# Strassen's scheme for the second token half of an encoder layer's input projection

## The chip, the cores and the metric

One core of one Trainium2 chip. The time is the device time of one execution in microseconds (us). The kernel is float32 throughout. Engines are named as the profile names them: PE is the tensor engine (PEld its weight loads), DVE the vector engine, ACT the scalar engine, POOL the GpSimd engine, SP the engine that issues most of the DMAs.

## The reference

One layer of a transformer-like encoder on 2048 tokens of width 1024 (`BATCH` 1, `DEPTH` 1), cut to what matters:

```python
h = rms_norm(x, norm_mix[l])
z = h @ w_in[l]                       # 1024 -> 4352
q_a, k_a, v_a, q_b, k_b, v_b, g_a, g_b = jnp.split(z, offsets, axis=-1)
                                      # 512, 128, 128, 512, 512, 512, 1024, 1024
y_a = windowed_gqa(q_a, k_a, v_a, sink[l])      # 8 heads on 2 kv heads, |t-s| <= 128, ALiBi
y_b = neighborhood_attn(q_b, k_b, v_b, rpb[l])  # 8 heads, 32 x 64 token grid, 8 x 16 window
gates = jax.nn.sigmoid(jnp.concatenate([g_a, g_b], axis=-1) + b_gate[l])
merged = gates[..., :D_MODEL] * (y_a @ w_proj_a[l]) + gates[..., D_MODEL:] * (y_b @ w_proj_b[l])
x = x + merged @ w_out[l]
x = x + jnp.square(jax.nn.relu(rms_norm(x, norm_mlp[l]) @ w_up[l])) @ w_down[l]
return rms_norm(x, norm_final)
```

## The kernel before

**Products in three parts.** Each float32 operand is split into a high and a low half (`split`, L234 to L236: ACT casts the high half, DVE or POOL subtracts it). Each 128 x 128 x 512 product is three matmuls, high-high, high-low and low-high (`mm3` at L193 to L195, `mm3s` at L239 to L241).

**Blocks and pages.** Tokens come in four blocks of 512 (0 to 3). The normalised input of a block is kept with features on partitions; a page is one half of the 1024 features for one block, 512 x 512, as a high and a low tile. A feature tile is 128 of the 4352 output columns.

**First token half: Strassen quads.** Blocks 0 and 1 are projected by a Winograd form of Strassen's scheme. `in_quad` (L407) takes two neighbouring groups of columns, `w` wide each (128 or 256), and both blocks; it makes seven products in the order `ORDER = (1, 2, 5, 6, 7, 4, 3)`, each of 12 matmuls for each of `w / 128` tiles. The left operands are sums of weight blocks (`in_left`, tiles `zS`, `zwhl`), the right ones seven pages `in_page[n]` (tiles `zh1` to `zh7`), made once from x. DVE adds the products up in `zc` tiles. The list of quads is

```python
QUADS = [(O_KA, P), (O_QA, 256), (O_QB, 256), (O_KB, 256), (O_VB, 256)]
QUADS += [(O_GA + n * BT, 256) for n in range(4)]
```

The first is a key and a value tile of attention A, the last four are the gates. `in_result` (L388) takes a finished tile: queries and keys are split once more (`qk_parts`, into an `in_e()` buffer, tile `ze`), values are transposed by PE and split (`v_parts`, L350 and L351, into `in_v2()`, tile `zv`, one buffer), and all are stored to DRAM by SP (`qs_a`, `ks_a`, `vs_a`, `qs_b`, `ks_b`, `vs_b`, `zg` for gates). Beside quads 4 and 5 (O_VB and the first gates) blocks 2 and 3 of x are normalised, transposed and stored to `h1d` (L448, L566).

**Attention A and B, with the second half as filler.** Then `h1d` is loaded again as four pages (`hT`), and the same 34 feature tiles of blocks 2 and 3 are made without Strassen, 24 matmuls a piece (`feature_tile`): `qk_tile`, `v_tile` and `gate_tile` are generators that yield after each block. Their 68 pieces are the filler of both attentions. `paced` ties each piece to the end of an attention unit:

```python
def paced(filler, pieces, total, lag):
    for n in pieces:
        at = n * 32 // total - lag
        with tc.issue_after(done[at]) if at >= 0 else nullcontext():
            next(filler, None)
```

Attention A has 32 units: kv group `g`, query block `i` (`attn_a`). A unit makes scores (L657, L658), adds a bias and takes the maximum (DVE L659), exponentials (ACT L666), scales by the reciprocal (POOL L670), transposes (PE L676), splits the transposed weights (ACT L679, DVE L680) and multiplies by the values (L681, L682). The filler for keys and queries is needed by later units, so A runs blocks 0 to 6 of both groups first (with 12 pieces), then 7 to 15 (with 12 more). Attention B has 32 units of head and column band (`attn_b`): scores L810, bias and maximum L815, exponentials L821, scale L825, transposes of four pairs of rows L837, split L842 and L843, products L848, output L855 and L856. 20 pieces are paced over B and 24 more issued behind the first loads of the merge.

**Merge and the rest.** For each block, `load_y` (L903, L904) loads and splits both attention outputs, the projections are gated and added, `w_out` is applied and the residual added. The result is normalised, transposed (L1182), scaled by ACT into an `h2s` tile (L1184, two buffers) and stored to `h2d`. The up and down projections follow, both by Strassen's scheme over all tokens.

**Order.** The program is written in one order; a scheduler in the framework then fixes each engine's own order at build time, within the data dependences and `issue_after`. Pools of on-chip memory are opened and closed as stacks on a left and a right side, so a tile may have to wait for the last user of the place that it takes.

Of the kernel before, what the change touches and what calls it, by code (L numbers as in the profile page):

```python
# [15 lines left out]
D = 1024  # L16
# [76 lines left out]
def encoder_layer(ctx, tc, x, norm_mix, w_in, b_gate, sink, rpb, w_pa, w_pb, w_out,  # L93
# [62 lines left out]
    h1d = [dp.tile([D, BT], F32, name=f"h1d{b}") for b in range(2)]  # L156
    zg = [[dp.tile([2, D, BT], F32, name=f"zg{b}")] for b in range(NB)]
# [114 lines left out]
    in_page = {n: ring(s_z, f"zh{n}", PAGE, F32R, 2, "left") for n in (1, 2, 6)}  # L272
# [4 lines left out]
    in_v2 = ring(s_z, "zv2", [P, 1024], F32, 1)  # L277
# [4 lines left out]
    in_page[3] = ring(s_z, "zh3", PAGE, F32R, 2)  # L282
    s_kv = ExitStack()
    kvw = ring(s_kv, "kvw", [P, 4, 256], F32, 2)
# [105 lines left out]
    def in_result(col, b, src, in_psum):  # L390

        if col < O_VB and col != O_VA:
            for dst, t in qk_parts(col, b, src, in_e()):
                SY.dma_start(dst, t)
            return
        if in_psum:
            t = in_e()[:, 0]
            A.copy(t, src)
            src = t
        if is_v(col):  # L400
            for dst, t in v_parts(col, b, src, zbank(tpool, 2), in_v2()):
                SY.dma_start(dst, t)
        else:
            f = (col - O_GA) // P
            SY.dma_start(zg[b][0][f // 8, (f % 8) * P : (f % 8 + 1) * P, :], src)

    def in_quad(c, w, lf, right, ybanks=ypool, zbanks=zpool):  # L407

        na = w // P
        x, y, z = [None] * 2, [None] * 2, [None] * 2  # L410
        c1, u2, c22 = [None] * 2, [None] * 2, [None] * 2
        for n in ORDER:
            hl, (rh, rl) = next(lf), right[n]
            for a in range(na):
                if n == 1:
                    x[a] = zbank(xpool[a])
                elif n == 5:
                    z[a] = zbank(zbanks[a])
                elif n == 6:
                    y[a] = zbank(ybanks[a])  # L420
                ps = {1: x, 2: x, 5: z, 3: z, 6: y, 7: y, 4: y}[n][a]
                at = slice(a * P, (a + 1) * P)
                for k in range(4):
                    mm3s(ps, hl[:, 0, k, at], hl[:, 1, k, at], rh[:, k], rl[:, k], k == 0 and n in (1, 5, 6), k == 3)
                first, second = c + a * P, c + w + a * P
                if n == 1:
                    c1[a] = in_c()
                    A.copy(c1[a], ps)
                elif n == 2:
                    in_result(first, 0, ps, True)  # L430
                elif n == 6:
                    u2[a] = in_c()
                    add(V, u2[a], ps, c1[a])
                elif n == 7:
                    c22[a] = in_c()
                    add(V, c22[a], ps, c1[a])
                    add(V, c22[a], z[a], c22[a])
                    in_result(second, 1, c22[a], False)
                elif n == 4:
                    add(V, c1[a], ps, c1[a])  # L440
                    in_result(second, 0, c1[a], False)
                elif n == 3:
                    add(V, u2[a], ps, u2[a])
                    in_result(first, 1, u2[a], False)
            yield
# [10 lines left out]
    def row_half(c, w, p):  # L456
        t = kvw() if w == P else in_raw()
        SY.dma_start(t, w_in[0][p * BT : (p + 1) * BT, c : c + 2 * w].rearrange("(k p) f -> p k f", p=P))
        return t
# [74 lines left out]
    xp = pools(s_z, "right", ("xin", "st"), "x2")  # L534
# [15 lines left out]
    for q in range(2, len(QUADS)):  # L550
        if q == 7:
            bias_tables()
        lf = list(in_left(ws, 256))
        if q + 1 < len(QUADS):
            ws = in_weights(*QUADS[q + 1])
        if q in (4, 5):

            b = q - 2
# [18 lines left out]
    s_h = ExitStack()  # L577
    hpl = [pool(f"hT{n}", side="left", stack=s_h) for n in range(4)]
# [3 lines left out]
    hp = {}  # L582
    for b in (2, 3):
        hi, lo = [], []
        for p in range(2):
            h, l = (T(hpl[2 * (b - 2) + p], PAGE, F32R, "hT", 2) for _ in range(2))
            for n, (hh, ll) in enumerate(zip(halves(h), halves(l))):
                raw = T(wp, [P, KC, P], F32, "raw", 3).rearrange("p (k a) c -> p k (a c)", k=2)
                r = p * BT + n * 256
                SY.dma_start(raw, h1d[b - 2][r : r + 256, :].rearrange("(k p) t -> p k t", p=P))  # L590
                split(raw, hh, ll, V)
            hi.append(h)
            lo.append(l)
        hp[b] = hi, lo


    def qk_tile(col, scale, tiled=False):
        hl = slice_of([(cols(w_in[0], col), KC)])
        yield
        for b in (2, 3):  # L600
            ps = psum("mm", 2)
            feature_tile(ps, hl, hp[b])
            out = qk_parts(col, b, ps, T(wp, [P, 2, BT], F32, "z", 2))
            for dst, t in out:
                SY.dma_start(dst, t)
            yield

    def v_tile(col):
        hl = slice_of([(cols(w_in[0], col), KC)])
        yield  # L610
        for b in (2, 3):
            ps = psum("mm", 2)
            feature_tile(ps, hl, hp[b])
            vt = T(wp, [P, 2, BT], F32, "z", 2)[:, 0]
# [7 lines left out]
    dist = T(ap_, [P, 384], F32, "dist", 1)  # L622
    SY.dma_start(dist, dist_a)
    bias_a = [None] * 2

    def make_bias_a(g):
        t = T(ap_, [P, 4, 384], F32, f"biasa{g}", 1)
        for h in range(4):
            G.tensor_scalar(t[:, h], dist, 2.0 ** -(4 * g + h + 1), 1.0, ALU.mult, ALU.mult)
        bias_a[g] = t  # L630
# [80 lines left out]
    def paced(filler, pieces, total, lag):  # L711

        for n in pieces:
            at = n * 32 // total - lag
            with tc.issue_after(done[at]) if at >= 0 else nullcontext():
                next(filler, None)

    def gate_tile(f, blocks):
        hl = slice_of([(cols(w_in[0], O_GA + f * P), KC)])
        yield  # L720
        for b in blocks:
            ps = psum("mm", 2)
            feature_tile(ps, hl, hp[b])
            z = T(wp, [P, 2, BT], F32, "z", 2)[:, 0]
# [12 lines left out]
    for g in (1, 0):  # L737
        make_bias_a(g)

    live = []  # L740
    for g in (1, 0):
        load_kv(g, 0)
# [13 lines left out]
    bp = pools(s_b, "right", ("masks", "braw", "biass", "biasl", "kb0", "qb", "kb1"), "b")  # L756
    bp.update(pools(s_b, "left", ("vb", "sb", "phb", "plb", "yb", "stb"), "b"))
    boff, bstart, btotal = bias_layout()
    masks = T(bp, [P, btotal], F32, "masks", 1)
# [125 lines left out]
    s_b.close()  # L885
    s_pg = ExitStack()
    p4 = pools(s_pg, "right", ("page", "yraw", "z"), "m")

    def load_y(b):
        yh, yl = [], []  # L890
        for n in range(2):
            h = T(p4, [P, 4, BT], F32R, "page", 4)
            l = T(p4, [P, 4, BT], F32R, "page", 4)
            for c in range(4):
                raw = T(p4, [P, BT], F32, "yraw", 6)
                src = (y_a[c // 2][(c % 2) * P : (c % 2 + 1) * P] if n == 0 else y_b[c])[:, b * BT : (b + 1) * BT]
                SY.dma_start(raw, src)
# [12 lines left out]
    paced(fill, range(20, 44), 40, 4)  # L910
# [227 lines left out]
    for b in range(NB):  # L1138
# [3 lines left out]
        for f in range(8):  # L1142
            hl = slice_of([(cols(w_pa[0], f * P), 4), (cols(w_pb[0], f * P), 4)])
            parts = []
            for n in range(2):
# [3 lines left out]
                g = T(wp, [P, 2, BT], F32, "z", 2)[:, 0] if n else T(p4, [P, BT], F32, "z", 4)  # L1149
# [7 lines left out]
            if b == 0:  # L1157
                load_wo(f)
# [20 lines left out]
        for k in range(KC):  # L1179
# [3 lines left out]
            ht = T(ph2, [P, BT], F32, "h2s", 2)  # L1183
# [214 lines left out]
```

## Time and profile before

| | |
|---|---|
| median of 3 runs | 2751.87 us (2751.0 to 2756.17) |
| the profiled execution | 2750.41 us, its span 2748.6 us |
| busy share of PE, DVE, ACT, POOL | 97%, 56%, 45%, 31% |
| dense projection matmuls (L193 to L195, `mm<-hT,whl`) | 3 x 544 |
| Strassen input matmuls (L239 to L241, `zb<-zh,zwhl`) | 3 x 476 |
| granted PE clock, mean | 0.986 |
| DMA | 480.86 MB, mean 175 GB/s |

Stages by the windows of the trace: the quads run to 387 us, attention A to 710, attention B to 1112, the merge to about 1500, up to 2131, down to the end. In a window's line the first figure is its length, then each engine's busy time with its number of instructions, then the granted clock (1.00 is full), the share of DMA time and GB/s. Matmuls are pipelined: one of 512 columns is shown as 0.39 us long, but the next starts 0.23 us after it, so the distance between starts is what a matmul costs.

### The profile page before, as it was taken

What the parts mean: (1) busy time and instruction counts of PE and PEld (TensorE: products, weight loads), DVE (VectorE), ACT (ScalarE), POOL (GpSimd) and SP (SyncE); (2) the same over time, 40 slices, a digit from 0 to 9 for tenths busy, and PEclk for the clock granted to TensorE, in tenths of its full rate; (3) what the DMA queues carried; (4) which work ended last, traced back from release to release, by engine and by line L of the source; (5) the groups of instructions that cost most, each with busy time, mean ns of one, the idle gap of its engine ahead of it and who ended that gap; (6) DMA issues with size and microseconds to landing.
All of it is one profiled execution on the core that took longest, in us unless ns stands there. A gap on an engine that the chain in (4) does not pass through costs nothing.

```text
span 2748.6 us, 35115 instructions
## 1 busy us (share of the span) xinstructions
PE 2658.3 (97%) x12332; PEld 2190.2 (80%) x12332; DVE 1551.9 (56%) x2352; ACT 1250.2 (45%) x2225; POOL 839.6 (31%) x671
## 2 busy tenths in 40 slices
PE   7998998999999999899999899989999999999998
PEld 6886877777788888787887788878888888888887
DVE  8754447676454444543435567586654644546667
ACT  6343236665455555534533444554444332322444
POOL 1111223334455552433420365555544000000000
PEclk9999999999999999999999999999999999999999
DMA  4855274446677665746534656574444954445555
GB/s 148 229 152 176 98 228 141 114 115 175 179 208 199 179 172 148 234 145 197 187 107 181 224 175 201 185 228 146 143 141 161 338 179 154 145 156 173 179 183 175
DMA packets 329664, 480.86 MB, mean 175 GB/s; under 512 B 28024, under 2 KB 162296, under 8 KB 327312
## 3 DMA queue, kind: packets, MB, share of 16 engines
q1 hardware_dynamic: 300560, 445.06, 51.5%
q10 hardware_dynamic: 28928, 33.56, 3.8%
q8 instruction: 97, 1.59, 0.2%
q14 instruction: 79, 0.65, 0.1%
HBM read 323.28 MB, written 155.26 MB: 174 GB/s over the span
## 4 chain that ended last, share of the span: by engine, by line
PE 85%; DMA 6%; DVE 5%; ACT 2%; issue 1%; POOL 0%; SPq 0%; ACTq 0%; POOLq 0%; DVEq 0%
PE b L239 14%; PE b L241 14%; PE b L240 14%; PE mm L193 5%; PE mm L195 5%; PE mm L194 5%; PE zb L241 3%; PE zb L240 3%; PE zb L239 3%; PE pt L193 2%; PE pt L195 2%; PE pt L194 2%; PE av L848 2%; PE pt L837 2%; PE s L810 2%
## 5 line engine op out<-in xcount | busy, mean ns | idle before, releaser
L240 PE MATMUL b<-dwh,dah 128*128 128x512 f32 x896 | 348.5, 389 | 0.0
L241 PE MATMUL b<-dwh,dah 128*128 128x512 f32 x896 | 347.7, 389 | 0.0
L239 PE MATMUL b<-dwh,dah 128*128 128x512 f32 x896 | 338.1, 389 | 1.5 <-ACT dwh L235 1.5
L232 POOL TENSOR_TENSOR uc<-uc,uc 128x512 f32<-128x512 f32 x120 | 233.3, 1958 | 206.8 <-issue 150.1
L235 ACT CAST dah<-da 128x1024 fp32r<-128x1024 f32 (+1 forms) x128 | 121.0, 945 | 366.4 <-PE b L241 243.1
L236 DVE TENSOR_TENSOR dah<-da,dah 128x1024 fp32r<-128x1024 f32 (+1 forms) x128 | 139.3, 1089 | 221.4 <-ACT dah L235 218.3
L239 PE MATMUL b<-ubh,uwhlb 128*128 128x512 f32 x592 | 232.2, 392 | 6.2 <-ACT h2s L1184 5.4
L241 PE MATMUL b<-ubh,uwhlb 128*128 128x512 f32 x592 | 231.3, 392 | 2.6 <-DVE uwhlb L236 2.6
L240 PE MATMUL b<-ubh,uwhlb 128*128 128x512 f32 x592 | 232.0, 392 | 0.0
L193 PE MATMUL mm<-hT,whl 128*128 128x512 f32 x544 | 220.7, 406 | 4.7 <-ACT whl L175 2.4
L232 DVE TENSOR_TENSOR uc<-b,uc 128x512 f32<-128x512 f32 x160 | 109.1, 688 | 203.1 <-PE b L241 162.6
L195 PE MATMUL mm<-hT,whl 128*128 128x512 f32 x544 | 217.0, 399 | 1.2 <-POOL whl L176 1.2
L194 PE MATMUL mm<-hT,whl 128*128 128x512 f32 x544 | 216.1, 397 | 0.0
L176 POOL TENSOR_TENSOR whl<-raw,whl 128x1024 fp32r<-128x1024 f32 x66 | 159.4, 2416 | 159.2 <-ACT whl L175 138.1
L1288 POOL TENSOR_TENSOR st<-st,power 128x1 f32<-128x1 f32 x16 | 13.6, 857 | 613.6 <-DVE st L1287 613.5
L239 PEld LDWEIGHTS b<-dwh,dah 128*128 128x128 f32 x896 | 168.1, 188 | 36.7 <-ACT dwh L235 1.9
L240 PEld LDWEIGHTS b<-dwh,dah 128*128 128x128 f32 x896 | 168.2, 188 | 34.9
L241 PEld LDWEIGHTS b<-dwh,dah 128*128 128x128 f32 x896 | 168.2, 188 | 34.8
L239 PE MATMUL zb<-zh,zwhl 128*128 128x512 f32 x476 | 190.4, 402 | 3.8 <-DVE zh L451 2.6
L240 PE MATMUL zb<-zh,zwhl 128*128 128x512 f32 x476 | 189.9, 400 | 1.8 <-DVE zh L236 1.8
L241 PE MATMUL zb<-zh,zwhl 128*128 128x512 f32 x476 | 187.5, 399 | 0.6 <-DVE zwhl L236 0.5
L239 PEld LDWEIGHTS b<-ubh,uwhlb 128*128 128x128 f32 x592 | 112.1, 189 | 30.2 <-ACT h2s L1184 5.7
(241 smaller groups left out, 6235.4 us busy)
## 6 DMA issues: line engine op xcount, KB each, us to landing
at<-uc SPq DMA_DIRECT2D x224, 256.0 KB
da<-at SPq DMA_DIRECT2D x96, 512.0 KB
dw<-in_w_down_dram SPq DMA_DIRECT2D x160, 256.0 KB
uraw<-in_w_up_dram SPq DMA_DIRECT2D x32, 1024.0 KB
raw<-in_w_in_dram SPq DMA_DIRECT2D x34, 512.0 KB
zraw<-in_w_in_dram SPq DMA_DIRECT2D x16, 1024.0 KB
z<-zg SPq DMA_DIRECT2D x64, 256.0 KB
xin<-in_x_dram SPq DMA_DIRECT2D x16, 512.0 KB
```

The costliest lines, as they stand in the source:

```text
L176: G.tensor_tensor(out=hl[:, 1], in0=raw, in1=hl[:, 0].bitcast(F32), op=ALU.subtract)
L193: PE.matmul(ps, lh, rh, start=first, stop=False)
L194: PE.matmul(ps, lh, rl, start=False, stop=False)
L195: PE.matmul(ps, ll, rh, start=False, stop=last)
L232: return eng.tensor_tensor(out=out, in0=a, in1=b, op=op).ins
L235: A.copy(hi, src)
L236: eng.tensor_tensor(out=lo, in0=src, in1=hi.bitcast(F32), op=ALU.subtract)
L239: PE.matmul(ps, lh, rh, start=first, stop=False, skip_group_check=True)
L240: PE.matmul(ps, lh, rl, start=False, stop=False, skip_group_check=True)
L241: PE.matmul(ps, ll, rh, start=False, stop=last, skip_group_check=True)
L810: PE.matmul(ps[:, :n], q[:, i, :], kv[:, z, B_R0[i] // 4 : (B_R0[i] + B_NR[i]) // 4, 4 * B_C0[j] : 4 * (B_C0[j] + w)], start=z == 0, stop= ...
L837: PE.transpose(pt[:kp, at + (i - i0) * P : at + (i - i0 + 1) * P], s[i][:, rr : rr + kp], ident)
```

## The change

The second half of the tokens goes through `in_quad` too, for the first four quads (keys, values and queries of A, queries and keys of B: 14 of the 34 feature tiles). Only `v_b` (4 tiles) and the gates (16) of blocks 2 and 3 stay dense filler: 40 pieces, 22 paced over A and 18 over B. The nine quads of the first half come first, then the four of the second; between them the seven pages are replaced, in the same memory, from `h1d` and from four sums of its blocks that are made in chunks beside quads 7 and 8 and kept in DRAM. Pages 1, 2 and 3 stay for the dense filler, which needs one more page (`b12`). Attention A runs group 0 whole, then group 1; its bias, K and V tiles are placed anew. The bias distances are loaded into the bias tile itself. O_VB's quad gets two value buffers of its own, x of blocks 2 and 3 is turned beside quads 5 and 6, two feature chunks to a store. Attention B is no longer cut in two; its mask has a pool of its own. In the merge the first load of `w_out` is issued after the first load of attention output, the `z` buffers become three single ones, and the last block's h2 goes into the merge's `mh` tile, eight chunks wide, instead of `h2s`.

```diff
-    in_page = {n: ring(s_z, f"zh{n}", PAGE, F32R, 2, "left") for n in (1, 2, 6)}
+    s_h = ExitStack()
+    in_page = {n: ring(s_h, f"zh{n}", PAGE, F32R, 2, "left") for n in (1, 2, 3)}
+    in_page[6] = ring(s_z, "zh6", PAGE, F32R, 2, "left")
...
-    in_v2 = ring(s_z, "zv2", [P, 1024], F32, 1)
+    in_v2 = [ring(s_z, "zv2", [P, 1024], F32, 1)]
...
-    def in_quad(c, w, lf, right, ybanks=ypool, zbanks=zpool):
+    def in_quad(c, w, lf, right, ybanks=ypool, zbanks=zpool, b0=0):
...
-                    in_result(first, 0, ps, True)
+                    in_result(first, b0, ps, True)
...
+    in_v2.append(ring(s_v, "zv3", [P, 1024], F32, 2))
...
+    steps = [(*c, 0) for c in QUADS] + [(*c, 2) for c in QUADS[:4]]
+    n_first = len(QUADS)
+    def chunk_sums(kk):
+        b = {}
+        for j, p in ((0, 0), (1, 0), (1, 1), (0, 1)):
+            b[p, j] = chunk()
+            SY.dma_start(b[p, j], h1d[j][p * BT + kk * P : p * BT + (kk + 1) * P, :])
+        t1, t3, t2, t4 = b[0, 0], b[0, 1], b[1, 1], b[1, 0]
+        for n, o, x, y in ((5, t1, t3, t1), (7, t3, t2, t3), (6, t2, t2, t1), (4, t4, t4, t2)):
+            add(V, o, x, y, ALU.subtract)
+            SY.dma_start(h1s_d[n][kk * P : (kk + 1) * P, :], o)
+    def next_page(n):
+        src = {1: h1d[0][0:BT], 2: h1d[0][BT:D], 3: h1d[1][BT:D]}.get(n)
+        src = h1s_d[n] if src is None else src
+        hi, lo = in_page[n](), in_page[n]()
+        for m, (h, l) in enumerate(zip(halves(hi), halves(lo))):
+            t = page_raw()
+            SY.dma_start(t, src[m * 256 : (m + 1) * 256, :].rearrange("(k p) t -> p k t", p=P))
+            split(t, h, l, G if n in (4, 3) else V)
+        right[n] = (hi, lo)
-    for q in range(2, len(QUADS)):
+    for q in range(2, len(steps)):
+        c, w, b0 = steps[q]
...
-        if q in (4, 5):
+        if q in (5, 6):
...
-            for k in range(KC):
-                ps = zbank(tpool, 2)
-                turned(ps, xt, k)
-                ht = in_e()[:, 0]
-                scaled(ht, ps, k)
-                SY.dma_start(h1d[b - 2][k * P : (k + 1) * P, :], ht)
-        for _ in in_quad(*QUADS[q], iter(lf), right):
+            for k in range(0, KC, 2):
+                ht = in_e()
+                for i in range(2):
+                    ps = zbank(tpool, 2)
+                    turned(ps, xt, k + i)
+                    scaled(ht[:, i], ps, k + i)
+                SY.dma_start(h1d[b - 2][k * P : (k + 2) * P, :].rearrange("(k p) t -> p k t", p=P), ht)
+        if q in (7, 8):
+            for kk in range(2):
+                chunk_sums(2 * (q - 7) + kk)
+        for _ in in_quad(c, w, iter(lf), right, b0=b0):
             pass
+        if q == n_first - 1:
+            s_ck.close()
+            page_raw = ring(s_z, "zpr", [P, 2, BT], F32, 4)
+            for n in ORDER:
+                next_page(n)
...
-    ap_ = pools(s_a, "left", ("ka1", "va1", "qa", "sa", "ph", "pl", "ya", "sta"), "a")
-    ap_.update(pools(s_a, "right", ("dist", "biasa0", "va0", "ka0", "biasa1"), "a"))
+    ap_ = pools(s_a, "left", ("ka1", "va1", "qa", "sa", "ph", "pl", "ya", "sta", "biasa1"), "a")
+    ap_.update(pools(s_a, "right", ("va0", "ka0", "biasa0"), "a"))
...
+    hp = {2: ([right[1][0], right[2][0]], [right[1][1], right[2][1]]),
+          3: ([b12[0], right[3][0]], [b12[1], right[3][1]])}
...
-        for n in pieces:
-            at = n * 32 // total - lag
+        for n in range(pieces):
+            at = min(n * 32 // total - lag, 31)
...
-    dense = [qk_tile(O_KA, 1.0), v_tile(O_VA)]
-    dense += [qk_tile(O_QA + t * P, 0.125) for t in range(4)]
-    for t in range(4):
-        dense.append(qk_tile(O_KB + t * P, 0.125))
-        dense.append(qk_tile(O_QB + t * P, 1.0, tiled=True))
-        dense.append(v_tile(O_VB + t * P))
-    fill = chain(dense + [gate_tile(f, (2, 3)) for f in range(16)])
+    fill = chain([v_tile(O_VB + t * P) for t in range(4)] + [gate_tile(f, (2, 3)) for f in range(16)])
...
-    drive((attn_a(g, i) for g in (1, 0) for i in range(7)), live, False)
-    paced(fill, range(12), 24, 3)
-    flush()
-    for g in range(2):
-        load_kv(g, 1)
-    drive((attn_a(g, i) for g in range(2) for i in range(7, 16)), live, True)
-    paced(fill, range(12, 24), 24, 3)
+    drive((attn_a(g, i) for g in range(2) for i in range(16)), live, True)
+    paced(fill, 22, 22, 3)
...
-    units = ahead_of(all_b(), 1)
-    drive((next(units) for _ in range(15)), live, False)
-    paced(fill, range(20), 40, 4)
-    flush()
-    drive(units, live, True)
+    drive(ahead_of(all_b(), 1), live, True)
...
     first_y = load_y(0)
-    paced(fill, range(20, 44), 40, 4)
+    first_load = last_dma[0]
+    paced(fill, 18, 14, 4)
...
-                load_wo(f)
+                with tc.issue_after(first_load):
+                    load_wo(f)
...
-            ht = T(ph2, [P, BT], F32, "h2s", 2)
+            if b == NB - 1:
+                h2 = T(p4x, [P, KC, BT], F32R, "mh", 1).bitcast(F32) if k == 0 else h2
+                ht = h2[:, k]
+            else:
+                ht = T(ph2, [P, BT], F32, "h2s", 2)
```

More of the change, by code (lines that the diff above doesn't have):

```diff
@@ L156, in encoder_layer @@
     h1d = [dp.tile([D, BT], F32, name=f"h1d{b}") for b in range(2)]
+    h1s_d = {n: dp.tile([BT, BT], F32, name=f"h1sum{n}") for n in (4, 5, 6, 7)}
     zg = [[dp.tile([2, D, BT], F32, name=f"zg{b}")] for b in range(NB)]
@@ L576, in encoder_layer @@
     wp = pools(s_w, "right", ("raw", "whl", "z", "v2"), "w")
-    s_h = ExitStack()
-    hpl = [pool(f"hT{n}", side="left", stack=s_h) for n in range(4)]
+    s_m = ExitStack()
+    masks = pool("masks", side="right", stack=s_m)
+    hpl = pool("hT", side="left", stack=s_h)
     s_a = ExitStack()
-    ap_ = pools(s_a, "left", ("ka1", "va1", "qa", "sa", "ph", "pl", "ya", "sta"), "a")
-    ap_.update(pools(s_a, "right", ("dist", "biasa0", "va0", "ka0", "biasa1"), "a"))
[L582 to L606, printed above, removed]
+    ap_ = pools(s_a, "left", ("ka1", "va1", "qa", "sa", "ph", "pl", "ya", "sta", "biasa1"), "a")
+    ap_.update(pools(s_a, "right", ("va0", "ka0", "biasa0"), "a"))
+    b12 = tuple(T(hpl, PAGE, F32R, "hT", 2) for _ in range(2))
+    for n, (h, l) in enumerate(zip(*map(halves, b12))):
+        raw = T(wp, [P, KC, P], F32, "raw", 3).rearrange("p (k a) c -> p k (a c)", k=2)
+        SY.dma_start(raw, h1d[1][n * 256 : (n + 1) * 256, :].rearrange("(k p) t -> p k t", p=P))
+        split(raw, h, l, V)
+    hp = {2: ([right[1][0], right[2][0]], [right[1][1], right[2][1]]),
+          3: ([b12[0], right[3][0]], [b12[1], right[3][1]])}
     def v_tile(col):
```

56 lines of the change are left out of this document (33 added, 23 removed).

## The prediction

> **What bounds the kernel now.** First the page: how full is each engine, and who is on the chain that ended last.
>
> ```profile
> PE 2658.3 (97%) x12332; PEld 2190.2 (80%) x12332; DVE 1551.9 (56%) x2352; ACT 1250.2 (45%) x2225; POOL 839.6 (31%) x671
> ```
>
> The tensor engine (PE) is busy for 97% of the span, and the page puts 85% of the last chain on it. So time changes in two ways only: matmuls that go away, and stretches in which PE stands still. Second, the windows by stage (us, then busy us and instruction counts of PE, PEld, DVE, ACT, POOL, then the granted clock):
>
> ```profile
> 0.00:387.00 387.00, 363.65 (x1599) 292.33 (x1600) 229.12 (x278) 157.90 (x240) 65.45 (x50) 0.99 0.55 164
> 387.00:710.00 323.00, 305.08 (x1517) 248.22 (x1516) 197.79 (x537) 186.50 (x462) 122.51 (x161) 0.98 0.55 148
> 710.00:1112.00 402.00, 393.24 (x2209) 338.26 (x2208) 192.51 (x496) 214.58 (x493) 192.21 (x212) 0.99 0.66 179
> ```
>
> These are the Strassen quads of the first half, attention A, attention B. In B the vector engine (DVE) and ACT have half of the time to spare, because 936 projection matmuls lie between the attention's own. Third, the waits of PE, longest first, from 230 to 1600 us (total, times, longest):
>
> ```profile
> PE s L193 <- ACT page L903: 8.3, 1, 8.3
> PE b L239 <- ACT h2s L1184: 5.4, 1, 5.4
> ...
> PE s L810 <- DMA qb<-qs_b: 4.6, 2, 3.1
> ...
> PE zb L229 <- ACT ze L448: 3.6, 1, 3.6
> ...
> PE zb L337 <- DVE zv L351: 2.4, 1, 2.4
> ...
> PE zb L229 <- DVE zv L351: 1.9, 1, 1.9
> ```
>
> These are joints between stages. A joint costs more than its wait, since a half-speed clock follows it. I call "lost" whatever a stretch takes beyond its matmuls at their usual distance from start to start (in the timeline 0.23 us for 512 columns, 0.177 for 384, 0.118 for 256, 0.109 for a transpose). By that count the span loses 137 us: 12 from 200 to 300 (v stores), 14 where A starts (387 to 430), 12 where B starts (700 to 740), 12 where the merge starts (1112 to 1130), 11 where the up projection starts (1500 to 1535).
>
> Fourth, single units of attention (windows from one unit's last product to the next one's):
>
> ```profile
> 459.20:467.10 7.90, 5.76 (x33) 4.83 (x32) 5.92 (x11) 4.37 (x8) 2.66 (x2) 1.00 0.52 135
> 467.10:470.50 3.40, 3.40 (x13) 2.99 (x11) 3.13 (x12) 1.99 (x8) 0.00 (x0) 0.50 0.35 90
> 533.70:540.00 6.30, 5.71 (x28) 3.79 (x28) 5.56 (x18) 4.74 (x13) 0.70 (x1) 1.00 0.70 187
> 540.00:548.30 8.30, 8.30 (x43) 6.87 (x43) 3.48 (x11) 5.06 (x13) 4.54 (x8) 1.00 0.13 38
> 641.50:648.10 6.60, 5.60 (x31) 3.93 (x29) 6.57 (x19) 4.72 (x13) 5.18 (x8) 1.00 0.64 169
> ```
>
> The third and fifth have no projection matmul in them, the first has 6, the fourth 24. Their own matmuls come to 4.4 to 5.3 us at the usual distances, so these thin units lose 1.9, 2.1 and 2.6; the filled one loses nothing. In a thin unit DVE is busy nearly throughout (6.57 of 6.60): PE waits for its own softmax. Of A's 29 units after the first, 5 are thin (at most 6 projection matmuls) and lose 1.97 each on average; the others lose 0.46. In B no unit has less than 24 (mean loss 0.3). This is the view that the change must be read by.
>
> **The parts.**
>
> *Matmuls gone.* 14 feature tiles x 2 token blocks x 24 matmuls = 672 dense ones become 7 products x 12 matmuls x 7 tile pairs = 588. 84 fewer x 0.231 us = -19.4. The Strassen quads run at the same distance as dense tiles (0.231 in both), so this is nearly certain. Their splits, sums and stores lie beside PE: the quads of the first half lose 0.1 to 0.2 us in 50 where no joint is near.
>
> *Filler gone from B.* What moves out of the attentions is their cover: 28 of 68 projection pieces. The order of the changed kernel's PE shows where the 40 pieces left stand: in A 8 thin units of 29, in B 17 of 31 with no filler at all and 14 with 24. No thin unit of B is in the trace, so I work one out. From the end of the transposes of its first pair, ACT makes one copy (0.48), then the four exponentials of a later unit, which stand next in its order:
>
> ```profile
> 735.88 0.54 ACT L821 ACTIVATE sb<-sb,stb 128x288 f32<-128x288 f32 x1 [1.75 <-DVE stb L818]
> ...
> 738.13 0.46 ACT L842 CAST phb<-pt 128x384 fp32r<-128x384 f32 x1
> ```
>
> 2.25 us for the narrow columns; 2 x (0.709 - 0.606) + 2 x (0.606 - 0.530) = 0.36 more for the wide ones, so 2.4. Then the copy of the previous output (0.5), DVE's sum of it (0.6, ACT's next copy beside it), DVE's low half (0.69): 4.8 with semaphores. PE meanwhile has four score matmuls and four products of the unit before (1.2), eight transposes (0.87), four scores (0.6) and four products (0.47): 3.1. It waits 1.7, with two smaller steps 2.0, as in A's rows. DVE needs 172 us for 30 units from 740 to 1090, at most 5.7 each, against 4.86 of PE: at least about 1 is lost per thin unit. Upper bound 3.5 (A's worst, 2.6, times four pairs over three chunks). I take 2.0, the hand sum and A's mean row together. So B loses 17 x 2.0 + 14 x 0.46 = 40 against 10 now: +31 (between +14 and +56). A: 8 x 1.97 + 21 x 0.46 = 25 against 21: +4 (0 to +10).
>
> *v stores.* O_VB's quad had one v buffer: ACT waited 29 us in it for stores. Now it has two, and the transposed x moves into the gate quads, in half as many stores. Of 12 lost, 9 go (4 to 12).
>
> *Start of A.* K and V of group 0 now lie where the last quad's weight halves lay, so their loads wait for that quad's last matmul. On SP four stores stand between them (0.57 us from issue to issue in the timeline of the v stores), so the last key half is issued near 4 us and, with 3 to 4.8 us to land (4.8 in the chain at 375), is there at 7 to 9; 24 projection matmuls (5.5) cover that but for some 2. The four page loads and splits ahead of the first dense tile become one. Two almost bare units follow as before. 14 lost become 8: -6 (-12 to +6).
>
> *Start of B.* Keys of B's first head come where A's group 0 was, long free; but its score tiles overlie A's last values, so PE still waits for one softmax: -3 (-8 to +5).
>
> *Start of the merge.* Two filler pieces (48 x 0.231 = 11.1 us) now stand between B's last product and the first merge product, and 12 products on A's output after them. Before, from that last product (1110.4) to the first product on B's output it took 13.2. 14 covers it: -11 (-12 to -3).
>
> *Start of up.* The last block's h2 has eight places instead of two, so ACT no longer waits for stores (5.6 us); but the place is that of the second up page, which now waits for the last store, and its products are put 24 matmuls later for it. Of 11, 5 go (-9 to +3).
>
> *Turn to the second half.* Seven pages are replaced while the last gate quad runs. A page is free 72 to 121 matmuls (16 to 27 us) before its successor is read; it needs two casts (1.05 each) and two differences (1.23 on DVE, 2.42 on POOL), its raw data are loaded ahead in four halves. On SP one gate store stands ahead of the last half. +1 (0 to +8).
>
> Sum: -19.4 + 31 + 4 - 9 - 6 - 3 - 11 - 5 + 1 = -17.4. The profiled execution took 2750.4 (span 2748.6 and 1.8 around it), 1.5 under the median 2751.9. So 2733 by the first, **2734** by the median.
>
> **Rivals.** (1) *Thin units let the clock drop* (slower). In the rows above the 2.3 us wait at 464 was followed by a window at clock 0.50; the waits of 1.9 and 2.1 us were not. If all 25 thin units were followed by 3.4 us at half speed, 1.7 each, that is +43: 2777. It decides from 10 dips on. Against it: one of five here. The Trainium skill, TensorE: Matmul & The Clock Gate, section on the second failure mode, warns of this pattern: where "the PE micro-idles between MM groups frequently enough that HAM oscillates", the half clock comes back between bursts. By that rule the change loses; the trace agrees with it in one unit of five.
>
> (2) *The stalls only move.* The 33 us saved at the joints rest on reused memory and on SP's order. If none of it comes, -17 + 33 = +16: 2768. Half of it: 2751. For it: three of the five joints wait for a buffer's earlier owner in the changed kernel too.
>
> (3) *B's softmax keeps up.* Thin units lose 1.0 as by DVE's load: 17 us less, 2717; with A's start and up at their best as well 2707. For it: ACT's exponentials may run before they are due.
>
> That the products were not saved is excluded: the changed order has 12,250 matmuls and transposes against 12,334.
>
> **How the numbers follow.** Forecast 0.54 (2720 to 2746); rival 3 0.13; rival 1 0.13; rival 2 whole 0.10, half 0.10. A difference of 0.2% (5.5 us) is what can be told from none. Faster: 0.54 + 0.13 = 0.67; within: the half case less a little, 0.09; slower 0.24. Of the range, 2708 takes in rival 3 and most of the joints' best; 2770 takes in rival 2, so that rival 1 and the tails stay out.
>
> **What would show it.** Per-unit windows in B: thin units near 6.9 us, PE waiting there for plb (DVE) and phb (ACT). Attention B near 285 us instead of 402, A near 290 instead of 323, the quads 135 longer. No wait on zv near 240, none over 2 us on page at the merge. The forecast is wrong if thin units of B lose over 3.0 us each (2.0 + 17.4 / 17, where the gain is used up), if the clock falls below 0.95 over B, or if a wait of over 5 us stands at the turn to the second half or at A's first scores.

## The result and the profile after

The changed kernel takes 2769.6 us (median of four runs, 2766.9 to 2775.8), the kernel before beside it 2752.05. The ratio is 1.0064, with a 95% interval of 1.0044 to 1.0084: 0.64% slower. The forecast was 2734, faster. The profiled execution took 2775.8 (span 2773.9), the slowest of the four and 6 us above the median; stages below are compared on spans, where the difference is 25.3 us (2773.9 against 2748.6). In the experiments one execution (4688 us at a mean clock of 0.73) was in a slow state and is left out of every figure.

The page's first line for the changed kernel; 84 matmuls and transposes are gone, and PE's share fell from 97% to 96%:

```profile
PE 2657.5 (96%) x12248; PEld 2181.0 (79%) x12248; DVE 1648.4 (59%) x2443; ACT 1274.8 (46%) x2252; POOL 836.1 (30%) x669
```

The windows of the quads, attention A and attention B of the changed kernel (length, busy us and counts by engine, granted clock):

```profile
0.00:524.90 524.90, 501.51 (x2193) 402.21 (x2194) 336.80 (x392) 213.48 (x309) 101.03 (x68) 0.99 0.65 188
524.90:820.00 295.10, 279.11 (x1423) 227.26 (x1422) 183.99 (x523) 181.99 (x459) 111.41 (x153) 0.98 0.48 141
820.00:1136.00 316.00, 268.93 (x1544) 230.66 (x1544) 189.56 (x485) 185.44 (x448) 157.82 (x197) 0.91 0.65 172
```

The quads are 138 us longer (135 forecast), A is 28 shorter and B 86 shorter, 316 where 285 was forecast. In B, PE is idle for 47 of 316 us and the clock is 0.91 instead of 0.99. The same count of "lost" time as in the prediction (a stage's length less its matmuls at their usual distances), made for whole stages, puts the difference in its place:

| stage | lost before | lost after | change | forecast |
|---|---|---|---|---|
| quads, from the first matmul | 31.2 | 32.4 | +1.2 | -9 + 1 = -8 |
| A | 36.5 | 31.6 | -4.9 | -6 + 4 = -2 |
| B | 20.8 | 85.8 | **+65.0** | +31 - 3 = +28 |
| merge | 23.2 | 12.5 | -10.7 | -11 |
| up and down | 1.4 | -4.5 | -5.9 | -5 |
| matmuls gone | | | -19.5 | -19.4 |
| sum | | | +25.2 | -17.4 |

The longest waits of PE from 230 to 1600 us in the changed kernel (total, times, longest):

```profile
PE av L869 <- DVE yb L877: 20.8, 15, 2.1
PE pt L858 <- DVE plb L864: 9.8, 7, 5.5
PE av L869 <- ACT phb L863: 9.0, 3, 4.5
PE s L690 <- DMA ks_b<-ze: 7.2, 1, 7.2
...
PE s L691 <- DMA ka<-ks_a: 3.7, 1, 3.7
PE zb L242 <- DVE zwhl L237: 3.7, 1, 3.7
```

The first three are in B; before, B had no wait for DVE or ACT over 2 us in all. Single units of B, from one unit's last product to the next one's:

```profile
851.60:858.30 6.70, 6.04 (x41) 4.80 (x39) 5.42 (x16) 4.61 (x12) 3.02 (x3) 1.00 0.26 74
858.30:868.60 10.30, 10.30 (x65) 9.15 (x63) 5.50 (x15) 6.53 (x15) 7.95 (x12) 1.00 0.60 131
868.60:883.50 14.90, 7.75 (x41) 7.09 (x39) 10.69 (x16) 5.58 (x15) 8.16 (x8) 0.66 0.81 247
883.50:890.90 7.40, 5.93 (x41) 4.85 (x39) 5.75 (x16) 4.93 (x13) 3.44 (x6) 1.00 1.03 221
```

The second has 24 projection matmuls and loses nothing. The first and the fourth have none and lose 1.7 and 2.5, about as forecast. The third has none either and loses 10.3. The 17 bare units (those without a projection matmul) lose 67.5 in all: 1.2 to 4.0 in twelve of them, 4.9 to 10.3 in five. The 14 covered ones, with 24 each, lose 7 in all.

Where did 8 us go at 868? The operation at L839 there negates and scales the maxima of the scores' rows, which the exponentials need; it is called the row maximum below. The vector engine and POOL in the changed kernel's timeline (start, duration, instruction):

```profile
868.13 6.19 DVE L839 TENSOR_SCALAR stb<-stb 128x4 f32<-128x4 f32 x1
```

```profile
868.21 2.34 POOL L177 TENSOR_TENSOR whl<-raw,whl 128x1024 fp32r<-128x1024 f32 x1
870.51 3.77 POOL L799 TENSOR_TENSOR biasl<-braw,masks_t 128x384 f32<-128x384 f32 x3
```

An operation on 128x4 numbers, 0.16 us in most units, takes 6.19: it ends 0.03 us after POOL's last bias sum. The low halves queued behind it on the vector engine came 6 us late, and PE waited 5.5 for them. A second outlier (9.2 lost, at 1000) is on ACT:

```profile
1008.89 0.53 ACTq L173 DMA_DIRECT2D y_b<-yb  x1
1009.52 0.97 ACT L863 CAST phb<-pt 128x512 fp32r<-128x512 f32 x2 [6.14 <-DMA braw<-tab]
```

ACT's store of an output, ready since 1003.5, was issued only at 1008.9, when a load of bias rows landed (the store's issue and POOL's use of those rows wait for the same semaphore); the casts that PE needed stood behind it.

### The profile page after: what moved, and what is told of

Read it like the earlier page. It is cut to its first block, busy times and chain, and to the rows that moved or that the text cites. A ratio compares the mean times of both kernels' runs of the same rounds, so it can differ in the third digit from the quotient of the medians.

```text
span 2773.9 us, 35174 instructions
## 1 busy us (share of the span) xinstructions
PE 2657.5 (96%) x12248; PEld 2181.0 (79%) x12248; DVE 1648.4 (59%) x2443; ACT 1274.8 (46%) x2252; POOL 836.1 (30%) x669
## 4 chain that ended last, share of the span: by engine, by line
PE 80%; DVE 7%; DMA 6%; ACT 4%; issue 2%; POOL 1%; SPq 0%; ACTq 0%; DVEq 0%; POOLq 0%
PE b L240 14%; PE b L242 14%; PE b L241 14%; PE zb L240 5%; PE zb L242 5%; PE zb L241 5%; PE mm L194 3%; PE mm L195 3%; PE mm L196 3%; PE av L869 2%; PE pt L194 2%; PE pt L196 2%; PE pt L195 2%; PE pt L858 1%; DMA z<-zg 1%
## 5 line engine op out<-in xcount | busy, mean ns | idle before, releaser
L240 PE MATMUL zb<-zh,zwhl 128*128 128x512 f32 x672 | 267.6, 401 | 8.7 <-DVE zc L233 3.8
L241 PE MATMUL zb<-zh,zwhl 128*128 128x512 f32 x672 | 267.7, 399 | 1.8 <-DVE zh L237 1.8
L242 PE MATMUL zb<-zh,zwhl 128*128 128x512 f32 x672 | 264.3, 399 | 4.6 <-DVE zwhl L237 4.5
L177 POOL TENSOR_TENSOR whl<-raw,whl 128x1024 fp32r<-128x1024 f32 x52 | 129.1, 2483 | 117.1 <-ACT whl L176 117.1
L240 PEld LDWEIGHTS zb<-zh,zwhl 128*128 128x128 f32 x672 | 127.5, 190 | 42.2 <-issue 4.6
L242 PEld LDWEIGHTS zb<-zh,zwhl 128*128 128x128 f32 x672 | 127.6, 190 | 35.5 <-DVE zwhl L237 5.9
L241 PEld LDWEIGHTS zb<-zh,zwhl 128*128 128x128 f32 x672 | 128.0, 191 | 31.2 <-DVE zh L237 2.1
L237 POOL TENSOR_TENSOR zwhl<-zraw,zwhl 128x1024 fp32r<-128x1024 f32 (+1 forms) x24 | 57.5, 2401 | 255.6 <-ACT zwhl L236 254.0
```

Source lines behind the costliest of these rows:

```text
L177: G.tensor_tensor(out=hl[:, 1], in0=raw, in1=hl[:, 0].bitcast(F32), op=ALU.subtract)
L237: eng.tensor_tensor(out=lo, in0=src, in1=hi.bitcast(F32), op=ALU.subtract)
L240: PE.matmul(ps, lh, rh, start=first, stop=False, skip_group_check=True)
L241: PE.matmul(ps, lh, rl, start=False, stop=False, skip_group_check=True)
L242: PE.matmul(ps, ll, rh, start=False, stop=last, skip_group_check=True)
```

## The experiments

All edits are to the changed kernel unless said otherwise. "B's loss" is the stage figure of the table. Times are medians; ratios are to the kernel before, run beside each, and are taken over all runs, so that they can differ a little from the ratio of the medians. Losses are of one profiled execution each, which can lie some us from the median.

**Cover in pieces of 12.** 28 of B's 32 units get 12 projection matmuls, instead of 24 or none. The tile's three matmuls go through `mm3s`, which makes the same three.

```diff
-            feature_tile(ps, hl, hp[b])
+            feature_tile(ps, hl, hp[b], range(KC // 2))
+            if halved:          # set after attention A
+                yield
+            feature_tile(ps, hl, hp[b], range(KC // 2, KC))
...
-    paced(fill, 18, 14, 4)
+    paced(fill, 36, 28, 4)
```

> The changed kernel with one edit: in attention B each gate tile is cut in two pieces of 12 matmuls, so that 28 of B's 32 units have 12 projection matmuls ahead of their products instead of 14 with 24 and 17 with none; the number of matmuls, the softmax work and all transfers are the same. Theory (a unit without cover waits for its own softmax chain, above all for the output copy and sum that free the one product bank): 12 matmuls are 2.8 us of cover against a typical wait of 1.7 us, so the covered units lose about 0.7 and the four bare ones 3 to 4; B's loss falls from 86 us to about 45, and the time from 2770 to about 2729 (2720 to 2740), under the kernel before. Rival (the loss is the total work of the softmax engines in B, no matter how the cover is spread): B's loss stays at 80 to 90 and the time at 2765 to 2775. Rival (the loss sits in the longer Strassen stage): the same 2765 to 2775.

Measured: 2767.8, ratio 1.0052 [1.0037, 1.0068]; B's loss 71.9. The timed runs can't tell it from the changed kernel. That is a miss for the theory as it stood, and the first rival, with a loss of 80 to 90, is not right either. The covered units still lose 1.6 on average, most of it in a few lumps of 3 to 8. PE's waits in B in this run:

```profile
PE av L875 <- ACT phb L869: 9.8, 8, 2.6
PE av L875 <- DVE yb L883: 8.3, 6, 2.1
```

The wait for `yb`, the ordinary one, fell from 20.8 to 8.3. The copies `phb` took its place: four of ACT's stores waited 0.8 to 3.5 us for a load's landing, as at 1008 above. And one row maximum took 4.6 us beside POOL's bias sums. So 2.8 us of cover hides much of the ordinary chain, but not these stops. The theory was widened: what the cover hid is the chain and, as much, the stops of the engines beside it.

**The row maximum on ACT**, to take the vector engine out of POOL's way.

```diff
-        V.tensor_scalar(nm, mx, -0.125, None, ALU.mult)
+        A.activation(nm, mx, AF.Copy, scale=-0.125)
```

> The changed kernel with one edit: in attention B the negated, scaled row maximum (128x4) is made by ACT instead of the vector engine. In the trace of the changed kernel this small operation takes 0.16 us as a rule but up to 6.2 us where a two-input operation of POOL runs beside it; 11.2 us in four of 29 cases. Theory (the vector engine stands still while POOL's operation holds something that both need, and in a unit without cover PE waits for it): the unit that lost 10.3 us loses about 3, some others 0.5 to 1 less; B's loss falls by 8 to 14 us, the time to 2756 to 2762. Rival (another vector operation waits for POOL in its place, or the wait was hidden): within 3 us of the changed kernel. Against the typical wait of 1.7 us this edit does nothing by either.

Measured: 2763.5, ratio 1.0048 [1.0036, 1.0060], just above the theory's range; B's loss 68.6. That is 6 us less by the medians, with intervals that overlap, and 13 by the profiled spans. The unit that lost 10.3 loses 2.7, as expected. 6.5 us of the 17 less are the unit at 1000 (9.2, now 2.7), which the edit does not touch: ACT's store met no late load there in this run. What is left in B is mainly the ordinary chain:

```profile
PE av L869 <- DVE yb L877: 14.5, 10, 2.0
PE s L831 <- DVE stb L836: 5.9, 8, 1.8
```

With this edit the 17 bare units lose 46 us, 2.7 each; the covered ones lose 12 instead of 7.

Two runs below, the pages on the vector engine and A's keys later, leave attention B as in the changed kernel, so their traces show what recurs. The long row maximum does, at the same unit (6.7 and 5.2 us there, 11.6 and 10.1 lost); ACT's late store is in neither. Their bare units lose 65 and 67 us, as many as in the changed kernel.

**The same edit in the kernel before**, the control.

> The kernel before with the one edit that its trace calls for as little as for any: the scaled row maximum of attention B on ACT. There too the operation took up to 1.5 us beside POOL (10 of 32 cases over 0.9). Theory (24 projection matmuls or more in every unit hide it): no change, within 4 us of the kernel before, where the same edit took 17 us of loss from B of the changed kernel. Rival (the vector engine's stops cost time with cover too): 4 to 8 us less.

Measured: 2752.2, ratio 1.0004 [0.9995, 1.0014]. No change, as the theory has it: with 23 matmuls or more in every unit the vector engine's stops cost no time that the runs can show. The trace does have less lost in B, 15 us against 21, so a few us of the stops may not be hidden; the rest of the span takes them up again.

**The last two pages on the vector engine**, at the turn to the second half.

```diff
-            split(t, h, l, G if n in (4, 3) else V)
+            split(t, h, l, V)
```

> The changed kernel with one edit: at the turn to the second token half the low halves of the last two pages (4 operations) are made by the vector engine (1.22 us each) instead of POOL (2.4 to 2.7 each). In the changed kernel PE stood 3.85 us at 382, and 1.0 twice near 396 and 400, for vector-engine operations that took 2.3 to 3.3 us beside POOL's instead of 1.2 to 1.5. Theory (they were stretched by POOL): these waits go, 5 to 8 us less, 2762 to 2765. Rival (the vector engine is simply too full there): 4.9 us more work for it, and the waits stay or grow: 2768 to 2776.

Measured: 2769.5, ratio 1.0060 [1.0047, 1.0073]; the timed runs can't tell it from the changed kernel. That is a miss for the theory's 2762 to 2765. The trace can tell: the loss from 350 to 420 us is 3.1 instead of 8.6 (8 to 10 in all six profiles of the changed kernel and its versions without the edit, 3 to 4 in all six with it). The vector engine there in the changed kernel, and then with the edit:

```profile
383.51 2.82 DVE L237 TENSOR_TENSOR zwhl<-zS,zwhl 128x512 fp32r<-128x512 f32 x1
386.37 3.29 DVE L233 TENSOR_TENSOR zS<-zraw,zraw 128x1024 f32<-128x1024 f32 x1
```

```profile
379.52 0.68 DVE L237 TENSOR_TENSOR zwhl<-zS,zwhl 128x512 fp32r<-128x512 f32 x1
381.86 1.22 DVE L233 TENSOR_TENSOR zS<-zraw,zraw 128x1024 f32<-128x1024 f32 x1
```

The same two operations take 0.68 and 1.22 when POOL does not run. Four of the fourteen page splits on POOL made these operations of the vector engine, which run beside them, three to four times as long.

**Keys and values of A later.** The loads of three of the four K and V parts are issued with units 5, 9 and 12.

```diff
-        for m in range(2):
-            load_kv(g, m)
-    drive((attn_a(g, i) for g in range(2) for i in range(16)), live, True)
+    drive(all_a(), live, True)    # load_kv(0, 0) ahead of unit 0, (0, 1), (1, 0), (1, 1) of 5, 9, 12
```

> The changed kernel with one edit: of the four loads of K and V for attention A (1.5 MB each) only the one that the first units read is issued at the start; the other three are issued with units 5, 9 and 12 of the first group. In the changed kernel PE waits 7.4 and 4.0 us at 530 and 538 for the first keys while the transfer engines are 90% busy with all four. Theory (the first keys wait behind later ones): both waits shrink, 6 to 10 us less, 2760 to 2764. Rival (the first keys wait for the last quad's end and for the stores ahead of them in SP's queue): the 7.4 us wait stays, at most 4 us are saved, 2766 to 2770; or a later load is late in turn, and nothing is saved.

Measured: 2772.9, ratio 1.0081 [1.0066, 1.0096]. The rival holds: the first wait stays,

```profile
PE s L690 <- DMA ks_b<-ze: 6.2, 1, 6.2
```

instead of 7.2. The second (3.7) is gone, but small waits for queries and weights came in turn, and A's loss is 30.9 against 31.6. The trace of the changed kernel shows what holds the first keys: the last quad's last matmul starts at 524.4, but SP issues their load only at 532.2, the last 3 us of it behind a wait for the semaphore of a store of B's keys (`ks_b`), and the first score, which waits for that load, starts at 537.7. With the later loads moved it is issued at 533.0, behind such a store again.

**Two banks for the products.**

```diff
-        po = psum("av", 1)
+        po = psum("av", 2)
...
-            ps = psum("s", 3)
+            ps = psum("s", 2)
```

> The changed kernel with one edit: two banks instead of one for the attentions' products, and two instead of three for the scores. Theory (in a unit without cover PE waits, 1.4 to 2.1 us each and 22 us in all over B, for the copy and the sum that free the only product bank): with a second bank the next unit's first products don't wait for them, these waits go or fall to what the next limit allows (the low half of the probabilities, 1.4 us where it ended last), B's loss falls from 86 by 10 to 22 us, 2750 to 2762. Rival (that wait only ended last by chance; exponentials, copies and low halves of the next unit stand right behind it, or the scores now wait for one of their two banks): B's loss stays within 6 us of 86, 2765 to 2775.

Measured: 2773.3, ratio 1.0081 [1.0064, 1.0098]; B's loss 74.8, but A's 35.5 and the quads' 34.6. The wait for `yb` is gone and two others stand in its place:

```profile
PE av L869 <- ACT phb L863: 16.8, 15, 2.5
PE av L869 <- DVE plb L864: 7.8, 22, 1.4
```

The bank only came last. Half of its 22 us was won in B, none in the total, so the theory missed the time and the rival, with a loss within 6 of 86, missed B; with one score bank less in the same edit, the two can't be told apart.

**Three edits together**: pieces of 12, row maximum on ACT, pages on the vector engine.

> The changed kernel with three edits together: cover in pieces of 12 in attention B, the 128x4 row maximum of B scaled by ACT, and the last two pages' low halves on the vector engine. One at a time they took B's loss from 86 us to 72 and to 69 and that of the Strassen quads from 32 to 25. If they add up: 14 + 17 + 7 = 38 us less, 2732 (2727 to 2742), under the kernel before. If the first two took away the same loss (the vector engine standing still in a bare unit): 17 + 7 = 24 less, 2746.

Measured: 2752.0, ratio 1.0000 [0.9986, 1.0013]; B's loss 61.1. They add up only in part: 18 us by the medians, where 38 were expected, or 24 if two of them took away the same. In the trace ACT's stores stopped it four times in B, by 1.2 to 4.9 us.

**And the stores of B on SP.**

```diff
-            A.dma_start(*pending.pop(0))
+            store_on[0].dma_start(*pending.pop(0))    # SY in attention B, for gates too
```

> The three edits together and a fourth: in attention B the stores of the outputs and of the gates are issued by SP instead of ACT. In the run with cover in pieces of 12, four of ACT's stores in B waited 1.2 to 3.5 us (in the changed kernel one waited 5.5) for a semaphore that ended with the landing of a load (keys, values, bias rows), and the probabilities' copies were queued behind them. Theory (those waits stop ACT and through it PE): 5 to 10 us less than the three edits alone. Rival (the same wait then stops SP, and the loads behind it come late): no gain, or up to 10 us more.

Measured: 2741.3, ratio 0.9968 [0.9957, 0.9980], 10.6 less than with three; B's loss 54.5. No store stops ACT in B any more. The rival may have a small part: a store of a gate now stops SP by 3.1 us, and PE waits for loaded queries twice in B, 6.0 us at the start (5.6 with three edits) and 3.4 at 994.

```profile
PE s L838 <- DMA qb<-qs_b: 9.3, 2, 6.0
```

With these four edits the changed kernel is faster than the kernel before.

**One quad of the four undone.** The keys of B are dense filler again, the rest as changed.

```diff
-    steps = [(*c, 0) for c in QUADS] + [(*c, 2) for c in QUADS[:4]]
+    steps = [(*c, 0) for c in QUADS] + [(*c, 2) for c in QUADS[:3]]
...
-    paced(fill, 18, 14, 4)
+    paced(fill, 26, 22, 4)
```

> The changed kernel with one part of the change undone: of the four quads of the second token half the last, the keys of attention B, is again made by dense tiles beside the attentions. That is 24 matmuls more (+5.5 us) and 8 pieces of cover more, which go to attention B: by the order of its PE 23 of B's 31 later units have 24 projection matmuls and 8 have none, instead of 14 and 17. Theory (a bare unit of B loses 4.1 us, a covered one 0.5, and this is what the change cost): 9 bare units fewer, 9 x 3.6 = 32 less loss in B, +5.5 for the matmuls: 2743 (2736 to 2752). Rival (the loss in B comes from POOL's and the stores' stops alone, whatever stands between): B's loss falls by at most 10 and the time stays at 2762 to 2772.

Measured: 2762.7, ratio 1.0035 [1.0021, 1.0048]; B's loss 55.2, 30.6 less. That is the theory's 32, and its bare units still lose 3.9 each. Of the gain, 5.5 pay for the matmuls and 5.6 are lost where A starts, where queries now come late (two waits of 3 us for `qa`, at 513 and 523). By medians 7 us are left, by the profiled spans 15; the theory's 2743 was too low.

**Four edits and that quad undone.**

> The four edits together (cover in pieces of 12, row maximum on ACT, last pages on the vector engine, stores of attention B on SP) and the keys of attention B dense: every unit of B then has 12 or 24 projection matmuls. Theory: the four bare units of the four edits lost 4.8 us each and the covered ones 0.96; with none bare and 8 pieces more of cover B's loss falls from 54 to about 35, less 5.5 for the matmuls: 14 us under the four edits alone, 2727 (2720 to 2736). Rival (the loss that is left in B is outliers that no cover hides): +5.5 and no gain, 2741 to 2748.

Measured: **2726.3, ratio 0.9909 [0.9895, 0.9923]**, under both kernels; B's loss 24.5. Every unit of B has 12 matmuls of cover or more. Attention B's window and PE's waits there:

```profile
783.00:1081.00 298.00, 287.22 (x1731) 249.87 (x1731) 172.38 (x453) 198.43 (x492) 171.74 (x202) 0.98 0.76 197
```

```profile
PE s L849 <- DMA kb<-ks_b: 5.2, 1, 5.2
PE av L887 <- ACT phb L881: 2.8, 1, 2.8
```

The clock is back at 0.98, and the wait for `yb` is gone from the list.

**Four edits and cover moved from A to B**, six pieces, with all four quads.

```diff
-    paced(fill, 22, 22, 3)
+    paced(fill, 16, 16, 3)
...
-    paced(fill, 36, 28, 4)
+    paced(fill, 48, 40, 4)
```

> The four edits together, and six of the 22 pieces of cover that stand in attention A go to attention B: A has 396 projection matmuls after its first unit instead of 504, B 468 instead of 324, and no unit of B is bare; matmuls in all as before the move. In the changed kernel A's units with at most 6 such matmuls lost 1.06 each, B's 4.1. Theory: B's loss falls from 54 to about 38, A gets 4 bare units more at 1.1: 11 us less than the four edits, 2730 (2723 to 2738). Rival (A's bare units cost more when they are every second one, as POOL and the vector engine have no time to catch up): A's loss rises by 10 to 20 and the time is 2741 to 2750.

Measured: 2731.0, ratio 0.9921 [0.9907, 0.9935]. B's loss falls by 26 to 28.3, A's rises by 13 to 43.1: both theory and rival see their part, and the sum is the theory's. The same cover is worth more in B than in A.

**The sigmoids later.** In the best version the last unit but one of B loses 4.8 with 24 matmuls in it.

```diff
+                with tc.issue_after(last_copy[0]) if b == 0 else nullcontext():
-                A.activation(g, g, AF.Sigmoid, bias=bg[:, 8 * n + f : 8 * n + f + 1])
+                    A.activation(g, g, AF.Sigmoid, bias=bg[:, 8 * n + f : 8 * n + f + 1])
```

> The four edits, the keys of attention B dense, and a sixth edit: the merge's first sigmoids on ACT are queued behind the last copy of attention B's probabilities. In the run without it ACT loads the sigmoid's table (1.28 us) and makes a sigmoid while the last unit but one waits for its copy; PE stands 3.0 us there and that unit loses 4.8. Theory (ACT's order, not the cover, makes this unit's loss; it has 24 projection matmuls): it loses less than 1.5, 3 to 5 us less in all, 2722 (2717 to 2727). Rival (the merge then waits for its sigmoids): the same or up to 5 us more.

Measured: 2726.4, ratio 0.9905 [0.9888, 0.9922]: no gain, where 3 to 5 us were expected. The unit still loses 4.3. ACT without the edit, and with it:

```profile
1057.31 1.28 ACT L1189 ACT_TABLE_LOAD   x1
```

```profile
1067.51 0.62 ACT L941 CAST page<-yraw 128x512 fp32r<-128x512 f32 x1 [1.48 <-DMA yraw<-y_b]
```

A page cast of the merge stands ahead of the same copy in ACT's order, and now waits for its load, so the copy is as late as before. That fits ACT's order as the cause; the sigmoid was not the only part of it.

## Why the prediction was wrong

**Matmuls gone**: right, -19.5 against -19.4. The second half's quads lose 0.1 us from 450 to 500 at the 0.231 us of the first.

**Filler gone from B**: the step that failed, as the term "17 thin units x 2.0". They lost 4.0 each, 67.5 in all instead of 34. Of the 43 us between the forecast and the profiled difference, 37 are B's. All three points of failure that the prediction set itself were passed: 3.0 for a thin unit, 0.95 for the clock (it was 0.91), and a wait of 5 us at A's first scores (it was 7.2). Why it was mis-sized can in part be read from the runs. With the vector engine out of POOL's way, the bare units lose 2.7 each, 46 in all. The 21 us between are put down to the stops, mainly the row maximum behind POOL. The store behind a load has 6.5 of them in this execution, but two traces without it lose as much in all. The hand sum went along one chain with every operation at its usual duration. It took the mean of an operation for granted, and the trace of before held the warning: the row maximum took over 0.9 us in 10 of 32 cases there, up to 1.5, which by the control cost no measurable time under cover. The upper bound of the term, +56 for B's units, was too low as well (+65). It was built on attention A's worst unit, and POOL makes nine of B's bias sums beside A and 77 beside B; that this is the reason is not shown.

**The other 0.7 of each bare unit**, 12 us in all, is put down to the clock, rival 1. In the run with the row maximum on ACT, matmuls slowed after waits cost 33 us in B, 13 more than before the change. In the changed kernel such matmuls cost 37 us in B against 20 before; the waits themselves grew from 11 to 53. So of +65, some 17 go with the half clock, as ten dips at the rival's 1.7 would cost, and 42 are standing still; the few us left are fewer matmuls below the usual distance. Rival 1 was right in kind and has about a quarter of the loss. The Trainium skill's page TensorE: Matmul & The Clock Gate, in its section on the second failure mode, says that frequent short waits bring the half clock back. B's 0.99 before and 0.91 after agree with it. Attention A, which has thin units too, kept 0.98.

**Rival 2**, that the joints' 33 us only move, did not come as a whole. Merge start -10.7 (forecast -11), up start -5.9 (-5) and the v stores -10 (-9; from 200 to 300 us 2.2 are lost instead of 12.3) came as forecast. A's start (-6) and B's start (-3) did not: PE waits 7.2 and 3.7 us for A's keys, and 3.5 for B's first queries where 4.6 stood before. The bounds of these two terms held, the values did not. The load of the later keys on the DMA engines was tried as the reason, and it is at most a small one (7.2 became 6.2); the load of the first keys is issued late, behind stores.

**Turn to the second half**: +1 forecast, +11 measured (8.6 from 350 to 420, 2.4 from 300 to 350). It was priced with casts and differences at their usual durations on both engines; side by side they took 2.3 to 3.3 us instead of 0.7 to 1.2. That is the vector engine stopped beside POOL, as at B's outliers, and the edit on it took away 5.5.

**Attention A**: +4 forecast for its units, -6 measured (14.6 lost in 29 units, 20.9 before); its units with at most 6 projection matmuls lose 0.8 to 1.8, not 1.97. This miss and that at the turn, 10 us each, cancel in the sum by luck.

Rival 3 (1.0 per thin unit) is excluded. What stays open: why the row maximum at 868 waited through five operations of POOL in a row when others got through after one, and how much of the two-bank run is owed to the score bank that it gave up.

## What to carry to other kernels

Before matmuls that fill another stage's gaps are taken away, price that stage bare, and not by the usual duration of its chain: look for the longest case of each small operation and each store's issue, because what hid them is what goes. Cover in small pieces left less lost in B than the same in large ones (72 us against 86 in the traces; the time alone does not show it), and cover was worth more beside the stage whose helpers stop each other. Here 5.5 us of extra matmuls took 31 us of loss from B, of which 7 (medians) to 15 (profiled spans) reached the time. Keep stores off the queue of an engine in the chain.

## What was not expected of the hardware

Some vector-engine operations that don't touch a product bank (the memory into which PE writes) stand still while POOL runs a two-input operation. The 128x4 row maximum takes 0.16 us as a rule, but 0.66 to 6.19 in ten of 32 cases of the changed kernel, each of them ending 0.02 to 0.03 us after one of POOL's; a 128x512 low half takes 0.69 alone and 2.82 beside POOL. The operations with a product bank as input (L836, L864, L877) kept their durations to 0.02 us throughout, and so did the reciprocal on the same 128x4 (0.17 to 0.18). The Trainium skill, SBUF — State Buffer, section "SBUF: two separate sides", tells of a port pair that the vector engine and GpSimd share as an exclusive lock, held for a whole instruction. The trace agrees in that the row maximum's waits end with an instruction of POOL's; where the page has one instruction, the 6.19 us case spans five.
